# A mixture of retrieved experts: the v product in plain float32 on four column groups, per quarter of 64 tokens

## The chip, the cores and the metric

One core of one Trainium2 chip runs the whole program. The metric is the device time of one execution in microseconds (us). The engines are TensorE (PE for its matmuls, PEld for its weight loads), VectorE (DVE), ScalarE (ACT), GpSimd (POOL) and SyncE (SP); 16 DMA engines move data.

## The reference

One encoder layer over 256 tokens of width 2048 (mixer, then a retrieval layer, all float32). The change is in the retrieval layer and in what prepares it:

```python
def peer_ffn(h, w_q, sub_keys, u_tab, v_tab):
    ...                                   # 8 heads x 16 experts of 16384 chosen per token, with a gate g
    def token_block(args):
        hx, ids, g = args
        u = u_tab[ids]
        a = jnp.einsum('td,tnd->tn', hx, u)
        act = jax.nn.gelu(a, approximate=False) * g
        return jnp.einsum('tn,tnd->td', act, v_tab[ids])
```

The output is `x + gate2 * peer_ffn(h2)`, normalised once more. An expert that no token chose has weight zero for every token, so the sums may also run over all experts, token by token, with a weight matrix `act` that is mostly zero.

## The kernel before

**Stages.** The mixer runs first. Then the queries and keys of the retrieval; then the *u stage*: the 16384 experts in 128 blocks of 128, each block's `u` loaded (SP), split into a float32r part `hu` and a remainder `lu` (ACT copies, DVE subtracts, lines 154 and 155), and multiplied with the hidden state in 48 matmuls of 256 columns (lines 169 to 173). Beside it run, as steps of generators paced by declared costs (`pay`), the choice of the experts (`side_steps`) and, from block 51 on, `sort_steps`. The products, through gelu and times the gate, go to a table `actd` in DRAM, one row of 256 tokens per expert; the last two blocks (`TAIL`) stay on chip.

**The sort.** `gmax` holds, per token tile of 128, whether an expert has any weight there (built in `oh_use`). `sort_steps` gives each expert one of four classes (only tile 0, both, only tile 1, none), ranks experts by class with small matmuls, and inverts the rank into the index `perm_idx`: block `b` of the sorted order is a list of 128 expert numbers. Fixed limits (`T0_TO`, `T1_FROM`, `T1_TO`) say which blocks are multiplied for which tile; `miss` is 1 if a class does not fit its limits.

**The v stage**, the subject here. Sorted blocks 0 to 108 are gathered by POOL: 128 rows of `peer_v` (1 MB, `rv`, line 1085) and their 128 rows of `actd` (128 KB, `mc`, line 1147), each by an indirect DMA with `perm_idx`. Fetches run `AHEAD` = 6 blocks ahead of the products, in POOL's queue in program order. For each block `v_block` splits the raw values into hi (ACT, line 1102) and lo (DVE, line 1103), splits the weights `mc` likewise (lines 159, 160), and adds into eight PSUM banks `po`, four of 512 columns for each token tile, three products (hi hi, lo hi, hi lo) of 128x128 weights and 512 moving columns: 12 matmuls per block and tile (line 1114). Blocks 0 to 79 count for tile 0, 28 to 108 for tile 1, so 161 (block, tile) pairs; blocks for both tiles and for one alternate, and the last four are for tile 1 alone. The two tail blocks go first (12 matmuls per tile). Six blocks before the end stands a branch (`values_load` and `tc.If`, lines 1175 to 1177): if `miss` is set, all the block and tile pairs left out are added as well.

**The end.** For each tile: `po` times the gate plus the stored `x` (lines 1190, 1191), square and sum (1197), the root and its refinement (179 to 185), the gain (1203), the scale (1207, 1209), the store (1210).

**Column groups.** One place of the kernel already addresses the array in groups of 32 columns, in `ada_q` at the start (line 353): plain float32, 32 weight columns, 512 moving columns, four at a time with four different moving slices:

```python
PE.matmul(prow[32 * j:32 * j + 32], lhsT=cact[:, k:k + 1].to_broadcast([128, 32]),
          rhs=raw[:, j], start=(k == ADA_PE[j]), stop=(k == ADA_PE[j + 4]),
          tile_position=(0, 32 * j))
```

The matmul of line 903 is plain float32 on the full array, 128x128 weights and 512 columns.

Of the kernel before, what the change touches and what calls it, by code (L numbers as in the profile page):

```python
# [9 lines left out]
F32 = mybir.dt.float32  # L10
F32R = mybir.dt.float32r
# [17 lines left out]
NBLK = 128  # L29
# [10 lines left out]
HPV = 0  # L40
T0_TO = 80
T1_FROM = 28
T1_TO = 109
# [3 lines left out]
AHEAD = 6  # L47
# [39 lines left out]
def hybrid_block_kernel(  # L87
# [642 lines left out]

    def a8(name, shape=(128, 8, 256), dt=F32):
        return ap_.tile(list(shape), dt, tag="A", name=name, bufs=ABUFS)
# [54 lines left out]
    gmax = [work[:, 2048 + 128 * i:2176 + 128 * i] for i in range(2)]  # L787
    stages = {}

    def oh_make(tt, q):  # L790
        t = tt * 128 + q * 4
        it = iota.unsqueeze(1).to_broadcast([128, 4, 128])
        ohs = []
        for i, src in enumerate((i2T, i1T)):
            oh = e2(f"oh{tt}_{q}") if i else work[:, 2304 + 512 * ((32 * tt + q) % 3):][:, :512]
            oh = oh.rearrange("p (t i) -> p t i", t=4)
            V.tensor_tensor(oh, it, src[:, t:t + 4].unsqueeze(2).to_broadcast([128, 4, 128]), ALU.is_equal)
            ohs.append(oh)
        for j in range(4):
            S.activation(ohs[1][:, j], ohs[1][:, j], AF.Copy, scale=gT[:, t + j:t + j + 1])  # L800
        return ohs

    def oh_use(tt, q, ohs):
# [10 lines left out]
        if qq == TB // 4 - 1:  # L814
            S.dma_start(gd[tt * (128 // TB) + tb], stage)
            if tb == 0:
                V.tensor_reduce(gmax[tt], stage, AX.X, ALU.max)
            else:
                mx = e2(f"mx{tt}_{tb}")[:, :128]
                V.tensor_reduce(mx, stage, AX.X, ALU.max)  # L820
                V.tensor_tensor(gmax[tt], gmax[tt], mx, ALU.max)
# [87 lines left out]
    def sort_steps():  # L909
        tri = work[:, 0:128]  # L910
        V.tensor_scalar(tri, iota, pidx, None, ALU.is_gt)
        cls = work[:, 128:640].rearrange("p (c i) -> p c i", c=4)
        for tt in range(2):
            V.tensor_single_scalar(gmax[tt], gmax[tt], 0.0, ALU.is_gt)
            V.memset(gmax[tt][:, NBLK - TAIL:], 0.0)
        V.tensor_tensor(cls[:, 1], gmax[0], gmax[1], ALU.mult)
        V.tensor_tensor(cls[:, 0], gmax[0], cls[:, 1], ALU.subtract)
        V.tensor_tensor(cls[:, 2], gmax[1], cls[:, 1], ALU.subtract)
        V.tensor_tensor(cls[:, 3], gmax[0], cls[:, 2], ALU.add)
        V.tensor_scalar(cls[:, 3], cls[:, 3], -1.0, 1.0, ALU.mult, ALU.add)  # L920
        yield 3.0
        pt = ps_tile("clstot")
        for c in range(4):
            keep(PE.matmul(pt[:, c:c + 1], lhsT=cls[:, c], rhs=ones[:, 0:1], start=True, stop=True))
        yield 5.0
        tot = work[:, 1408:1416]
        keep(V.tensor_copy(tot[:, 0:4], pt[:, 0:4]))
        yield 3.0
        keep(PE.matmul(pt[:, 8:12], lhsT=ones, rhs=tot[:, 0:4], start=True, stop=True))
        yield 5.0  # L930
        keep(V.tensor_copy(tot[:, 4:8], pt[:, 8:12]))
        yield 3.0
        pr = ps_tile("rank")
        keep(PE.matmul(pr, lhsT=tri, rhs=cls.rearrange("p c i -> p (c i)"), start=True, stop=False,
                      skip_group_check=True))
        for c in range(4):
            for k in range(c + 1):
                keep(PE.matmul(pr[:, c * 128:(c + 1) * 128], lhsT=tot[:, k:k + 1].to_broadcast([128, 128]),
                              rhs=tri if k == c else ones, start=False, stop=(c == 3 and k == 3),
                              skip_group_check=True))  # L940
        yield 5.0
        rk = e2("rk")
        keep(V.tensor_tensor(rk, cls.rearrange("p c i -> p (c i)"), pr, ALU.mult))
        rank = work[:, 640:1024].rearrange("p (c i) -> p c i", c=3)
        V.tensor_reduce(rank[:, 0], rk.rearrange("p (c i) -> p i c", c=4), AX.X, ALU.add)
# [8 lines left out]
        lim = work[:, 1416:1420]  # L954
        V.tensor_scalar(lim[:, 0:1], tot[:, 4:5], -1.0, 128.0 * T1_FROM, ALU.mult, ALU.add)
        V.tensor_tensor(lim[:, 1:2], tot[:, 4:5], tot[:, 5:6], ALU.add)
        V.tensor_tensor(lim[:, 2:3], lim[:, 1:2], tot[:, 6:7], ALU.add)
        V.tensor_single_scalar(lim[:, 1:2], lim[:, 1:2], -128.0 * T0_TO, ALU.add)
        V.tensor_single_scalar(lim[:, 2:3], lim[:, 2:3], -128.0 * T1_TO, ALU.add)
        V.tensor_reduce(lim[:, 3:4], lim[:, 0:3], AX.X, ALU.max)  # L960
        V.tensor_single_scalar(lim[:, 3:4], lim[:, 3:4], 0.0, ALU.is_gt)
        V.tensor_copy(miss, lim[:, 3:4])
# [127 lines left out]
    turn = [0]  # L1090

    def hi_lo(name):
        k = turn[0]
        turn[0] += 1
        if k % 4 < 2:
            return [wp.tile([128, 2048], F32R, tag="w" + x, name=f"{x[0]}v{name}") for x in ("hi", "lo")]
        return spare[:, k % 2], cst.tile([128, 2048], F32R, tag="T3" + "ab"[k % 2], name=f"lv{name}")

    def v_block(raw, w, av, mm, tts, start=(), stop=()):
        hi, lo = w  # L1100
        with tc.high_priority(offset=HPV):
            S.activation(hi, raw, AF.Copy)  # L1102
            V.tensor_tensor(lo, raw, hi.bitcast(F32), ALU.subtract)  # L1103
        mh, ml = mm
        cs = slice(tts[0] * 128, (tts[-1] + 1) * 128)
        split_to(av[:, cs], mh[:, cs], ml[:, cs])
        for tt in tts:
            tsl = slice(tt * 128, (tt + 1) * 128)
            terms = list(enumerate(((mh, hi), (mh, lo), (ml, hi))))
            order = [(t, d4) for t in terms for d4 in range(4)]  # L1110
            if tt in stop:
                order = [(t, d4) for d4 in range(4) for t in terms]
            for (i, (lhs, rhs)), d4 in order:
                PE.matmul(po[tt * 4 + d4], lhsT=lhs[:, tsl], rhs=rhs[:, d4 * 512:(d4 + 1) * 512],  # L1114
                          start=(tt in start and i == 0), stop=(tt in stop and i == 2))

    units = []
    rest = []
    for b in range(NBLK):
        tts = [b < T0_TO, T1_FROM <= b < T1_TO]  # L1120
        units.append((b, [tt for tt in range(2) if tts[tt]]))
        rest.append((b, [tt for tt in range(2) if not tts[tt]]))
    both = [u for u in units if len(u[1]) == 2]
    ones_ = [u for u in units if len(u[1]) == 1]
    rest = [u for u in rest if u[1]]
    main = []
    late = ones_[-LATE:]
    ones_ = ones_[:-LATE]
    while both or ones_:
        if both:  # L1130
            main.append(both.pop(0))
        if ones_:
            main.append(ones_.pop(0))
    main += late

    tails = [v_raw(i - TAIL, f"d{i}") for i in range(TAIL)]
    raws, ms = [], []

    def fetch_raw(n):
        if n < len(main):  # L1140
            raws.append(v_raw(main[n][0], f"{main[n][0]}"))
# [6 lines left out]

    for n in range(AHEAD - TAIL):
        fetch_raw(n)  # L1150
    for n in range(AHEAD - TAIL):
        fetch_m(n)
    spare = None
    for i in range(TAIL):
        v_block(tails[i], hi_lo(f"d{i}"), ab[-1][:, ABLK - TAIL + i],
                [m1(f"m{x}d{i}", F32R) for x in "hl"], (0, 1), start=(0, 1) if i == 0 else ())
    final = {}
    for n, (b, tts) in enumerate(main):
        for tt in tts:
            final[tt] = n  # L1160
    spare = cst.tile([128, 2, 2048], F32R, tag="T1", name="hvs")
    gfin = None
# [3 lines left out]
    for n, (b, tts) in enumerate(main):  # L1166
        for k in ((AHEAD - TAIL + n * 2, AHEAD - TAIL + n * 2 + 1) if n < TAIL else (n + AHEAD,)):
            fetch_raw(k)
            fetch_m(k)
        if n % 4 == 0:  # L1170
            mm = wp.tile([128, 4, 2, 256], F32R, tag="wraw", name=f"mm{n}", bufs=WRAW)
        v_block(raws[n], hi_lo(f"{b}"), ms[n // 8][:, n % 8], (mm[:, n % 4, 0], mm[:, n % 4, 1]), tts,
                stop=[tt for tt in tts if final[tt] == n])
        if n == len(main) - 1 - AHEAD:
            flag = nc.values_load(miss[0:1, 0:1], min_val=0, max_val=1)
            xr = a8("xr", (128, 2048))
            with tc.If(flag > 0):
                xm = e2("xm")
                xs = [sp.tile([128, 512], F32R, tag="e2", name=f"xs{i}", bufs=E2BUFS) for i in range(2)]
                for rb, rtts in rest:  # L1180
                    nc.gpsimd.indirect_dma_start(xr, None, v_rows, index(rb))
                    nc.gpsimd.indirect_dma_start(xm[:, :256], None, actd[:, :], index(rb))
                    v_block(xr, hi_lo(f"x{rb}"), xm[:, :256], xs, rtts)
            gfin = a8("gfin", (128, 2048))
            nc.sync.dma_start(gfin, g_final.partition_broadcast(128))

# [37 lines left out]
def _consts():  # L1224
# [13 lines left out]
    mats = np.zeros((128, 2, 128), f)  # L1238
# [62 lines left out]
```

## Time and profile before

| | |
|---|---|
| median of 3 runs | 1894.97 us (1893.25 to 1897.15) |
| profiled execution, its own time | 1894.67 us |
| its span, first to last instruction | 1892.7 us |
| mean granted TensorE clock | 0.975 |
| TensorE / DVE / ACT / POOL busy | 95% / 73% / 49% / 20% |
| v stage, line 1114: first and last matmul start | 1414.4 and 1878.9 us |

Busy shares are means over the span; what a stage waits for has to be read in that stage. A matmul's record runs from its start to the end of its drain, so records overlap: the cost of one in a stream is the distance between starts, not its duration. A plain float32 matmul leaves two records.

### The profile page before, as it was taken

To read this page: it belongs to the slowest core of one execution; us is meant where nothing else is said; L and a number is where in the kernel's file an instruction comes from. 1 tells how busy PE (TensorE), PEld (TensorE's weight loads), DVE (VectorE), ACT (ScalarE), POOL (GpSimd) and SP (SyncE) were. 2 spreads that over 40 slices of the span, in tenths; PEclk is the share of its full clock that TensorE was granted. 3 is DMA by queue.
4 is the path that set the end of the run, shared out by engine and by line. 5 is a ranking of instruction groups with operands and counts; after the bars stand their busy time and mean duration, and the time that the engine had idled before them with its cause. 6 is when DMAs were issued, how large, how long until landed. Compare 5 with 4: busy or idle time off the path is not lost. (4 is left out here: it accounts for less than half of the span.)

```text
span 1892.7 us, 30584 instructions
## 1 busy us (share of the span) xinstructions
PE 1795.0 (95%) x12863; PEld 1675.1 (89%) x12863; DVE 1385.6 (73%) x1707; ACT 924.4 (49%) x1163; POOL 371.4 (20%) x257
## 2 busy tenths in 40 slices
PE   4878999899999998998999999999999999999995
PEld 2668999899999998998999999999998888888884
DVE  7568879888678977988657788876456665666666
ACT  3214457345544488578733334334345555555544
POOL 0000000000000000000000000000028887777760
PEclk8888999999999999999999999999999999999998
DMA  9976968789644555556597888888668888888781
GB/s 394 383 288 246 354 234 338 280 304 348 231 170 171 193 186 187 188 188 217 188 327 274 302 275 302 296 297 327 239 235 303 325 307 291 273 288 300 277 299 68
DMA packets 77794, 506.00 MB, mean 267 GB/s; under 512 B 9328, under 2 KB 9968, under 8 KB 22352
## 3 DMA queue, kind: packets, MB, share of 16 engines
q1 hardware_dynamic: 44640, 319.79, 45.5%
q0 software_dynamic: 29712, 162.94, 25.1%
q10 hardware_dynamic: 3296, 21.24, 2.8%
q8 instruction: 102, 1.67, 0.3%
q14 instruction: 44, 0.36, 0.1%
HBM read 466.18 MB, written 37.75 MB: 266 GB/s over the span
## 5 line engine op out<-in xcount | busy, mean ns | idle before, releaser
L169 PE MATMUL pu<-h2hi,hu 128*128 128x256 f32 x2048 | 500.3, 286 | 0.0
L154 ACT ACTIVATE hu<-ru 128x2048 fp32r<-128x2048 f32 x128 | 245.4, 1917 | 367.9 <-PE pu L170 326.0
L155 DVE TENSOR_TENSOR lu<-ru,hu 128x2048 fp32r<-128x2048 f32 x128 | 292.9, 2289 | 170.1 <-ACT hu L154 168.4
L169 PEld LDWEIGHTS pu<-h2hi,hu 128*128 128x128 f32 x2048 | 387.7, 189 | 0.6 <-issue 0.2
L173 PE MATMUL pu<-h2hi,lu 128*128 128x256 f32 x2048 | 263.0, 281 | 0.0
L170 PE MATMUL pu<-h2loT3a,hu 128*128 128x256 f32 x1024 | 252.0, 284 | 0.0
L173 PEld LDWEIGHTS pu<-h2hi,lu 128*128 128x128 f32 x2048 | 251.3, 188 | 0.0
L170 PE MATMUL pu<-h2loT3b,hu 128*128 128x256 f32 x1024 | 248.2, 281 | 0.0
L1013 POOL DMA_DIRECT2D gg<-gd x16 | 18.7, 1171 | 938.2 <-DMA gd<-stage 938.2
L170 PEld LDWEIGHTS pu<-h2loT3a,hu 128*128 128x128 f32 x1024 | 195.4, 191 | 0.2 <-issue 0.2
L170 PEld LDWEIGHTS pu<-h2loT3b,hu 128*128 128x128 f32 x1024 | 193.4, 189 | 0.0
L1147 POOL DMA_INDIRECT mc<-actd,perm_idx x109 | 184.3, 1691 | 33.2 <-issue 32.6
L1114 PE MATMUL po<-lv,mm 128*128 128x512 f32 x644 | 176.3, 394 | 1.4 <-DVE lv L1103 1.4
L1114 PE MATMUL po<-hvs,mm 128*128 128x512 f32 x648 | 170.0, 397 | 0.0
L1103 DVE TENSOR_TENSOR lv<-rv,hv 128x2048 fp32r<-128x2048 f32 x54 | 123.8, 2294 | 62.6 <-ACT hv L1102 61.0
L1114 PE MATMUL po<-hv,mm 128*128 128x512 f32 x640 | 164.7, 392 | 4.3 <-ACT hv L1102 4.3
L1103 DVE TENSOR_TENSOR lv<-rv,hvs 128x2048 fp32r<-128x2048 f32 x55 | 126.0, 2295 | 56.7 <-ACT hvs L1102 56.6
L1085 POOL DMA_INDIRECT rv<-in_peer_v_dram,perm_idx x109 | 153.1, 1405 | 62.2 <-issue 23.5
L1114 PEld LDWEIGHTS po<-hvs,mm 128*128 128x128 f32 x648 | 122.3, 189 | 29.4
L1114 PEld LDWEIGHTS po<-hv,mm 128*128 128x128 f32 x640 | 120.6, 189 | 30.5 <-ACT hv L1102 4.8
L1114 PEld LDWEIGHTS po<-lv,mm 128*128 128x128 f32 x644 | 121.4, 189 | 29.6 <-DVE lv L1103 2.0
L159 ACT ACTIVATE mm<-mc 128x256 fp32r<-128x256 f32 (+1 forms) x109 | 39.2, 361 | 191.9 <-DMA mc<-actd,perm_idx 191.8
(523 smaller groups left out, 3332.5 us busy)
## 6 DMA issues: line engine op xcount, KB each, us to landing
ru<-in_peer_u_dram SPq DMA_DIRECT2D x128, 1024.0 KB, 5.3
ada<-in_w_ada_dram SPq DMA_DIRECT2D x96, 1024.0 KB, 6.1
rwin<-in_w_in_dram SPq DMA_DIRECT2D x33, 1024.0 KB, 6.5
rwout<-in_w_out_dram SPq DMA_DIRECT2D x16, 1024.0 KB, 5.4
rwq<-in_w_q_dram SPq DMA_DIRECT2D x16, 1024.0 KB, 5.2
gd<-stage ACTq DMA_DIRECT2D x16, 1024.0 KB, 5.1
gg<-gd POOLq DMA_DIRECT2D x16, 1024.0 KB, 11.3
actd<-A POOLq DMA_DIRECT2D x15, 1024.0 KB, 6.4
```

The costliest lines, as they stand in the source:

```text
L154: S.activation(hi, raw, AF.Copy)
L155: V.tensor_tensor(lo, raw, hi.bitcast(F32), ALU.subtract)
L159: S.activation(hi, src, AF.Copy)
L169: PE.matmul(dst, lhsT=whi[:, sl], rhs=rhi[:, c], start=(c == sets[0][0]), stop=False)
L170: PE.matmul(dst, lhsT=whi[:, sl], rhs=rlo[:, c], start=False, stop=False)
L173: PE.matmul(dst, lhsT=wlo[:, sl], rhs=rhi[:, c], start=False, stop=(c == sets[-1][-1]))
L1013: keep(nc.gpsimd.dma_start(gg, gd[:, :, k * ABLK:(k + 1) * ABLK, :].rearrange("tb p i t -> p tb i t")))
L1085: keep(nc.gpsimd.indirect_dma_start(raw, None, v_rows, index(b)))
L1103: V.tensor_tensor(lo, raw, hi.bitcast(F32), ALU.subtract)
L1114: PE.matmul(po[tt * 4 + d4], lhsT=lhs[:, tsl], rhs=rhs[:, d4 * 512:(d4 + 1) * 512], start=(tt in start and i == 0), stop=(tt in stop and i ...
L1147: keep(nc.gpsimd.indirect_dma_start(ms[-1][:, n % 8], None, actd[:, :], index(main[n][0])))
```

## The change

It does five things.

1. **Products.** In the v stage, raw float32 values are used as they come from the DMA; the hi and lo parts, their tiles and the splits of the weights are gone. A product is made per sorted block and *quarter* of 64 tokens: the quarter's 64 weight columns are two groups of 32, each a matmul of 128x32 weights and 512 columns on its own column group of the array (`tile_position`), for four 512-column slices.
2. **Order.** A plan pairs a product of an even quarter (column groups 0, 1) with one of an odd quarter (groups 2, 3); the matmuls of a pair are issued slice by slice, four groups each. The blocks' order is chosen so that even and odd products keep level and about one block is used per pair.
3. **Sort.** `gmax` is kept per quarter, experts fall in 15 classes (every non-empty set of quarters) in the order of `QCLASSES`, whose pairs are the block windows allowed for each class. Compares, totals, ranks and limits follow; class tables and matmuls are bfloat16.
4. **Buffers.** Raw blocks use 11 buffers (7 `A`, 4 `wraw`) with fetches 8 ahead and 5 before the tails; the tails are loaded into `wraw` by SP; `xr` and `gfin` use the freed `whi`.
5. **The branch** stands where the fetches have all been asked for, and the last two pairs are merged slice by slice, so that the PSUM banks finish one after the other.

```diff
-T0_TO = 80
-T1_FROM = 28
-T1_TO = 109
+QCLASSES = ((7, 0, 6), (5, 4, 13), (13, 10, 17), (9, 15, 24), (1, 22, 36), (3, 32, 42), (2, 40, 53),
+            (10, 51, 60), (11, 57, 65), (15, 62, 68), (14, 66, 73), (6, 70, 80), (4, 77, 91),
+            (12, 88, 98), (8, 95, 109))
+NSORT = max(hi for _, _, hi in QCLASSES)
-AHEAD = 6
+EARLY = 5
+AHEAD = 8
+RAWS = 11
...
+        for k in range(nk):
+            V.tensor_single_scalar(cls[:, k], key, float(order[k]), ALU.is_equal)
+        yield 4.0
...
+        for k4 in range(0, nk, 4):
+            pr = ps_tile(f"rank{k4}")
+            keep(PE.matmul(pr, lhsT=tri, rhs=cls[:, k4:k4 + 4].rearrange("p k i -> p (k i)"), start=True, stop=False,
+                          skip_group_check=True))
+            for k in range(4):
+                keep(PE.matmul(pr[:, k * 128:(k + 1) * 128], lhsT=tot[:, k4 + k:k4 + k + 1].to_broadcast([128, 128]),
+                              rhs=tri, start=False, stop=(k == 3), skip_group_check=True))
+            yield 5.0
...
-    def v_block(raw, w, av, mm, tts, start=(), stop=()):
-        hi, lo = w
-        with tc.high_priority(offset=HPV):
-            S.activation(hi, raw, AF.Copy)
-            V.tensor_tensor(lo, raw, hi.bitcast(F32), ALU.subtract)
...
+    late = [u for u in steps if u[1] == 3][-2:] + [u for u in steps if u[1] == 12][-LATE:]
...
+    def halves(need):
+        return [q for q in (0, 2) if need >> q & 1], [q for q in (1, 3) if need >> q & 1]
...
+    def product(raw, m, q, d4, stop=False):
+        for s in range(2):
+            g, j = 2 * q + s, 2 * (q % 2) + s
+            bank = q // 2 * 4 + d4
+            PE.matmul(po[bank][32 * j:32 * j + 32], lhsT=m[:, 32 * g:32 * g + 32],
+                      rhs=raw[:, d4 * 512:(d4 + 1) * 512], start=(bank, j) not in seen, stop=stop,
+                      tile_position=(0, 32 * j))
+            seen.add((bank, j))
+
+    def v_raw(n, name):
+        if n % RAWS in (2, 5, 8, 10):
+            return wp.tile([128, 2048], F32, tag="wraw", name=f"rv{name}", bufs=WRAW)
+        return a8(f"rv{name}", (128, 2048))
...
     for i in range(TAIL):
...
+        for q0 in (0, 2):
+            for d4 in range(4):
+                for q in (q0, q0 + 1):
+                    product(tails[i], ab[-1][:, ABLK - TAIL + i], q, d4)
...
+    while i < n_pairs:
+        group = pairs[i:i + 1] if i < n_pairs - 2 else pairs[i:]
+        fetch_to(max(n for p in group for n, _ in p) + AHEAD)
+        for d4 in range(4):
+            for k, p in enumerate(group):
+                for n, q in p:
+                    product(raws[n], ms[n // 8][:, n % 8], q, d4, stop=ends[q] == i + k)
+        if i == at_if:
             flag = nc.values_load(miss[0:1, 0:1], min_val=0, max_val=1)
...
```

## Rows read from the trace of the kernel before

**Rows 1.** Part 1 of the page: busy us (share of the span) and instructions.

```profile
PE 1795.0 (95%) x12863; PEld 1675.1 (89%) x12863; DVE 1385.6 (73%) x1707; ACT 924.4 (49%) x1163; POOL 371.4 (20%) x257
```

**Rows 2.** Stretches: us, busy (count) of PE, PEld, DVE, ACT, POOL, PEclk, DMA share, GB/s.

```profile
1250.00:1300.00 50.00, 50.00 (x426) 49.68 (x424) 36.49 (x28) 18.30 (x18) 4.08 (x4) 1.00 0.81 282
...
1414.00:1854.00 440.00, 439.99 (x1913) 358.48 (x1911) 272.00 (x215) 228.12 (x215) 333.28 (x215) 1.00 0.83 294
1854.00:1880.00 26.00, 19.61 (x72) 15.07 (x72) 23.45 (x28) 15.85 (x18) 0.00 (x0) 0.87 0.01 3
```

**Rows 3.** Line 1114: count, duration ns min/median/max, first and last start.

```profile
L1114 PE MATMUL po<-hvs,mm x648: 395/396/628, 1425.3 to 1878.9; 128*128 128x512 f32 x162
...
L1114 PE MATMUL po<-hvd,mhd x16: 389/389/398, 1414.4 to 1423.3; 128*128 128x512 f32 x16
```

**Rows 4.** Order of time, PE around the If: start, us, instruction, wait before.

```profile
1852.92 1.07 PE L1114 MATMUL po<-hv,mm 128*128 128x512 f32 x4
1858.32 1.35 PE L1114 MATMUL po<-hv,mm 128*128 128x512 f32 x4 [4.33 <-ACT hv L1102]
1861.05 2.08 PE L1114 MATMUL po<-lv,mm 128*128 128x512 f32 x4 [1.38 <-DVE lv L1103]
```

**Rows 5.** DMA from 1430 to 1840 us: packets, MB, share; issues, landing us.

```profile
q0 software_dynamic: 19773, 121.50, 83.7%
...
rv<-in_peer_v_dram,perm_idx POOLq DMA_INDIRECT x104, 6.5
mc<-actd,perm_idx POOLq DMA_INDIRECT x103, 5.2
```

**Rows 6.** Order of time, PE and PEld near 46 and 53 us.

```profile
46.61 0.16 PEld L353 LDWEIGHTS adarow<-ada,cact 128*32 128x32 f32 x8
46.61 1.06 PE L353 MATMUL adarow<-ada,cact 128*32 128x512 f32 x8
...
47.61 0.39 PE L625 MATMUL pin<-hhi,hwin 128*128 128x256 f32 x1
...
53.48 1.92 PE L353 MATMUL adarow<-ada,cact 128*32 128x512 f32 x16
```

**Rows 7.** Order of time, PE at line 903.

```profile
1359.84 3.60 PE L903 MATMUL gtfp<-gtf,ones 128*128 128x512 f32 x8
```

**Rows 8.** POOL's gathers, lines 1085 and 1147: duration ns, starts.

```profile
L1085 POOL DMA_INDIRECT rv<-in_peer_v_dram,perm_idx x109: 933/944/3035, 1408.9 to 1839.2; - x109
...
L1147 POOL DMA_INDIRECT mc<-actd,perm_idx x109: 942/996/3066, 1414.9 to 1840.5; - x109
```

**Rows 9.** Groups by line in the u stage, and the index's last step.

```profile
L970 PE MATMUL inv<-sv,sl 128*128 128x256 bf16 x128 | 19.5, 275 | 0.0
...
L155 DVE TENSOR_TENSOR lu<-ru,hu 128x2048 fp32r<-128x2048 f32 x74 | 169.5, 2290 | 133.5 <-ACT hu L154 131.7 <-ACT A L1045 1.6 <-PE inv L970 0.2
...
L993 DVE CAST perm_idx<-work x1: 228/228/228, 1294.8 to 1294.8; 128x128 uint32<-128x128 f32 x1
```

**Rows 10.** Order of time, the end of the kernel.

```profile
1881.89 1.28 DVE L1191 TENSOR_TENSOR oacc<-oacc,ev 128x512 f32<-128x512 f32 x2
...
1883.24 0.58 ACT L1197 ACTIVATE po<-oacc 128x512 f32<-128x512 f32 x1
1883.76 0.19 ACT L1197 ACTIVATION_READ_ACCUMULATOR po<-oacc 128x1 f32 x1
1884.90 0.15 DVE L1199 TENSOR_REDUCE fsum<-fs 128x1 f32<-128x4 f32 x1
...
1886.76 1.15 ACT L1207 ACTIVATE oacc<-oacc,fr1r 128x1024 f32<-128x1024 f32 x1 [0.81 <-DVE fr1r L185]
...
1887.94 0.34 ACTq L1210 DMA_DIRECT2D out_dram<-oacc  x1
```

**Rows 11.** Line 353: duration ns of its weight loads.

```profile
L353 PEld LDWEIGHTS adarow<-ada,cact x128: 105/108/178, 19.9 to 140.8; 128*32 128x32 f32 x128
```

**Rows 12.** Order of time, PE from 19 us.

```profile
19.94 3.34 PE L353 MATMUL adarow<-ada,cact 128*32 128x512 f32 x16
```

More of the change, by code (lines that the diff above doesn't have):

```diff
@@ L786, in hybrid_block_kernel @@
     work = cst.tile([128, 4096], F32, tag="T2", name="work")
-    gmax = [work[:, 2048 + 128 * i:2176 + 128 * i] for i in range(2)]
+    gmax = [work[:, 2048 + 128 * i:2176 + 128 * i] for i in range(4)]
     stages = {}
@@ L921, in sort_steps @@
         yield 3.0
+        for k in range(nk):
+            V.tensor_single_scalar(cls[:, k], key, float(order[k]), ALU.is_equal)
+        yield 4.0
         pt = ps_tile("clstot")
-        for c in range(4):
-            keep(PE.matmul(pt[:, c:c + 1], lhsT=cls[:, c], rhs=ones[:, 0:1], start=True, stop=True))
+        for k in range(nk):
+            keep(PE.matmul(pt[:, k:k + 1], lhsT=cls[:, k], rhs=ones_bf[:, 0:1], start=True, stop=True))
         yield 5.0
-        tot = work[:, 1408:1416]
-        keep(V.tensor_copy(tot[:, 0:4], pt[:, 0:4]))
+        keep(V.tensor_copy(tot, pt[:, 0:nk]))
@@ L928, in sort_steps @@
         yield 3.0
-        keep(PE.matmul(pt[:, 8:12], lhsT=ones, rhs=tot[:, 0:4], start=True, stop=True))
+        keep(PE.matmul(pt[:, 32:32 + nk], lhsT=ones_bf, rhs=tot, start=True, stop=True))
         yield 5.0
-        keep(V.tensor_copy(tot[:, 4:8], pt[:, 8:12]))
-        yield 3.0
[L933 to L945, printed above, removed]
+        ends = [work[:, 1440 + nk * i:1440 + nk * (i + 1)] for i in range(2)]
+        sums = work[:, 1440 + 2 * nk:1440 + 3 * nk]
+        keep(V.tensor_copy(sums, pt[:, 32:32 + nk]))
+        src = sums
+        for i, d in enumerate((1, 2, 4, 8)):
+            V.tensor_copy(ends[i % 2][:, :d], src[:, :d])
+            V.tensor_tensor(ends[i % 2][:, d:], src[:, d:], src[:, :nk - d], ALU.add)
+            src = ends[i % 2]
@@ new lines, in sort_steps @@
+        starts = ends[0]
+        V.tensor_tensor(starts, src, sums, ALU.subtract)
+        over = work[:, 1664:1696]
+        V.tensor_tensor(over[:, 0:nk], lims[:, 0:nk], starts, ALU.subtract)
+        V.tensor_tensor(over[:, nk:2 * nk], src, lims[:, nk:2 * nk], ALU.subtract)
+        V.tensor_reduce(work[:, 1696:1697], over, AX.X, ALU.max)
+        V.tensor_single_scalar(work[:, 1696:1697], work[:, 1696:1697], 0.0, ALU.is_gt)
+        V.tensor_copy(miss, work[:, 1696:1697])
+        yield 3.0
@@ new lines, in sort_steps @@
+        rank = work[:, 1664:2048].rearrange("p (c i) -> p c i", c=3)
+        for k4 in range(0, nk, 4):
[6 more added lines that the diff above has]
+            yield 5.0
+            rk = e2(f"rk{k4}")
+            for k in range(4):
+                op = V.scalar_tensor_tensor(rk[:, k * 128:(k + 1) * 128], pr[:, k * 128:(k + 1) * 128],
+                                            starts[:, k4 + k:k4 + k + 1], cls[:, k4 + k], ALU.add, ALU.mult)
+                if k == 0:
+                    keep(op)
+            dst = rank[:, 1] if k4 else rank[:, 0]
+            V.tensor_reduce(dst, rk.rearrange("p (c i) -> p i c", c=4), AX.X, ALU.add)
+            if k4:
+                V.tensor_tensor(rank[:, 0], rank[:, 0], rank[:, 1], ALU.add)
@@ L1117, in hybrid_block_kernel @@
[L1117 to L1124, printed above, removed]
+    steps = []
+    for b in range(NSORT):
+        need = 0
+        for m, lo, hi in QCLASSES:
+            if lo <= b < hi:
+                need |= m
+        steps.append((b, need))
@@ L1125, in hybrid_block_kernel @@
+    rest = [(b, 15 & ~(steps[b][1] if b < NSORT else 0)) for b in range(NBLK)]
     rest = [u for u in rest if u[1]]
+    late = [u for u in steps if u[1] == 3][-2:] + [u for u in steps if u[1] == 12][-LATE:]
+    left = [u for u in steps if u not in late]
     main = []
[L1127 to L1133, printed above, removed]
-    main += late
-    tails = [v_raw(i - TAIL, f"d{i}") for i in range(TAIL)]
+    odd = taken = 0
@@ new lines, in halves, with unlike @@
+    def halves(need):
+        return [q for q in (0, 2) if need >> q & 1], [q for q in (1, 3) if need >> q & 1]
+    while left:
+        def unlike(u):
+            e, o = halves(u[1])
+            return (abs(odd + len(o) - len(e)) + abs(2 * (len(main) + 1) - taken - len(e) - len(o)), u[0])
+        u = min(left, key=unlike)
+        left.remove(u)
+        e, o = halves(u[1])
+        odd += len(o) - len(e)
+        taken += len(e) + len(o)
+        main.append(u)
+    main += late
+    pairs = []
@@ new lines, in hybrid_block_kernel @@
+    for part in (range(len(main) - len(late)), range(len(main) - len(late), len(main))):
+        lanes = [[(n, q) for n in part for q in halves(main[n][1])[i]] for i in range(2)]
+        for i in range(max(len(x) for x in lanes)):
+            pairs.append([lane[i] for lane in lanes if i < len(lane)])
+    n_pairs = len(pairs)
+    seen = set()
+    def product(raw, m, q, d4, stop=False):
[6 more added lines that the diff above has]
+            seen.add((bank, j))
@@ L1137, in hybrid_block_kernel @@
+    def v_raw(n, name):
+        if n % RAWS in (2, 5, 8, 10):
+            return wp.tile([128, 2048], F32, tag="wraw", name=f"rv{name}", bufs=WRAW)
+        return a8(f"rv{name}", (128, 2048))
+    tails = []
+    for i in range(TAIL):
+        raw = load_raw(peer_v[NBLK - TAIL + i], f"rvd{i}")
+        tails.append(raw)
     raws, ms = [], []
@@ L1147, in fetch_m @@
             keep(nc.gpsimd.indirect_dma_start(ms[-1][:, n % 8], None, actd[:, :], index(main[n][0])))
-    for n in range(AHEAD - TAIL):
+    for n in range(EARLY):
         fetch_raw(n)
-    for n in range(AHEAD - TAIL):
+    for n in range(EARLY):
         fetch_m(n)
-    spare = None
     for i in range(TAIL):
[L1155 to L1162, printed above, removed]
+        for q0 in (0, 2):
+            for d4 in range(4):
+                for q in (q0, q0 + 1):
+                    product(tails[i], ab[-1][:, ABLK - TAIL + i], q, d4)
     oacc = cst.tile([128, 2, 2048], F32, tag="T2", name="oacc")
@@ L1165, in hybrid_block_kernel, with fetch_to @@
         nc.sync.dma_start(oacc[:, tt], xd[tt])
[L1166 to L1174, printed above, removed]
+    gfin = None
+    asked = EARLY
+    at_if = next(i for i, p in enumerate(pairs) if max(n for n, _ in p) + AHEAD >= len(main) - 1)
+    ends = {}
+    for i, p in enumerate(pairs):
+        for n, q in p:
+            ends[q] = i
+    def fetch_to(n):
+        nonlocal asked
+        while asked <= min(n, len(main) - 1):
+            fetch_raw(asked)
+            fetch_m(asked)
+            asked += 1
+    i = 0
+    while i < n_pairs:
[3 more added lines that the diff above has]
+            for k, p in enumerate(group):
+                for n, q in p:
+                    product(raws[n], ms[n // 8][:, n % 8], q, d4, stop=ends[q] == i + k)
+        if i == at_if:
             flag = nc.values_load(miss[0:1, 0:1], min_val=0, max_val=1)
[L1176 removed]
+            xr = load_tile("xr")
             with tc.If(flag > 0):
                 xm = e2("xm")
[L1179 to L1180 removed]
+                for rb, need in rest:
                     nc.gpsimd.indirect_dma_start(xr, None, v_rows, index(rb))
                     nc.gpsimd.indirect_dma_start(xm[:, :256], None, actd[:, :], index(rb))
[L1183 to L1184 removed]
+                    for q in range(4):
+                        if need >> q & 1:
+                            for d4 in range(4):
+                                product(xr, xm[:, :256], q, d4)
+            gfin = load_tile("gfin")
             nc.sync.dma_start(gfin, g_final.partition_broadcast(128))
+        i += len(group)
     def add_up(po, j, tt, name):
```

71 lines of the change are left out of this document (26 added, 45 removed).

## The prediction

> **What bounds the kernel now.** I read the page's busy shares first. TensorE is busy 95% of the span, no other engine more than 73% [rows 1]; so the question for each stage is whether TensorE waits there. The table by stretches comes next. In the u stage and from 1414 to 1854 us TensorE is busy the whole time at the full granted clock (1.00, the 2.4 GHz level) [rows 2]. The first v matmul starts at 1414.4 and the last at 1878.9 [rows 3]; with 0.40 us for the last one the v stage is 464.9 us long. Its cost is a plain rate: 1913 matmuls in 440 us are 0.230 us each, and 161 (block, token tile) pairs x 12 plus 48 for the two tail blocks are 1980, so 455.4 us. The other 9.5 us lie at 1854 to 1866: TensorE stops after the If (4.33 us until ACT's hi, then 1.38 until DVE's lo) and four matmuls then take 2.08 us where they took 1.07 before, at a granted clock of 0.87 for the stretch [rows 2, 4]. Thirdly the DMA: 83.7% of its engines' time in the v stage [rows 5], so not the bound, but the next one. The end, from 1879.3 to 1892.7, is 13.4 us of DVE, ACT and the store.
>
> **What replaces the matmuls.** Twelve float32r matmuls per block and 128 tokens become, per block and quarter, eight float32 matmuls of 32 columns: two column groups x four 512-column slices. Even quarters (0, 2) use groups 0 and 1, odd ones (1, 3) groups 2 and 3, so a pair of one even and one odd product gives four sets of four matmuls side by side. Counting the class windows by the diff's own loop, the quarters need 53, 54, 53 and 57 blocks: 106 even, 111 odd, hence 111 pairs, five of them with the odd half alone (same time). With the tails, 2 blocks x 2 pairs x 4 sets, there are 111 x 4 + 16 = 460 sets.
>
> **The price of a set.** The trace has this operation elsewhere: line 353 runs plain float32 128x512 on four column groups of 32, each group with its own moving data. Eight records (each float32 matmul leaves two) span 1.06 us, and a run of sixteen spans 1.92 [rows 6]: the second set adds 0.86. A float32 matmul on the full array, line 903, takes 3.60 us for four [rows 7], so the four groups really run at once. I take 0.86 us: 460 x 0.86 = 395.6 us. Below, the same sixteen records leave no room under about 0.85; above, the single set's 1.06 if nothing overlaps between sets, which is one of the rivals.
>
> **The splits go.** 109 ACT copies, as many DVE subtractions and the small splits vanish from the stage. They ran beside TensorE, so this by itself gives nothing, except where TensorE waited for them: the 4.33 and 1.38 us behind the If, and the half-rate matmuls after. What is late there next is the branch alone: TensorE's queue must run empty and refill. No row isolates that; it lies between 0.3 and 4.3 us [rows 4]. I take 1, since the 4.33 is put down to ACT's hi, which is gone. Stage: 395.6 + 1.0 = 396.6 us, 68.3 less.
>
> **DMA.** The blocks fetched stay 109, a row gather of 1 MB and one of 128 KB each. From 1430 to 1840, 104 and 103 of them took 83.7% of 410 us, 343 us, 3.32 us a block at full use [rows 5]. A pair takes 3.44 us and the plan uses about one block per pair, so the DMA would be some 95% busy and TensorE stay ahead of nothing: 109 x 3.32 = 362 us against 111 x 3.44 = 382. The gathers begin at 1408.9 as now [rows 8]; the tails keep TensorE until 1414.4 + 13.8 = 1428.2, by when 5.8 blocks fit and one is needed. The 11 raw buffers let POOL ask eight ahead. POOL's issues take 0.94 to 1.00 us at the median and up to 3.1 [rows 8]; 218 of them at 1.25 with the 0.3 between are 272 us, so its queue does not bind. Nothing else waits behind them on POOL. What the deeper look-ahead costs the DMA no row shows: at worst the cadence of today, 410/103.5 = 3.96 us a block, at best 3.32.
>
> **Start, sort, end.** The tails' loads use the weight buffers of the last u blocks on SP's queue instead of A buffers; they need no split, and their first product still waits for u block 127 on TensorE, so 1414.4 stays. The sort adds on DVE 16 compares, 16 PSUM multiplies and 3 more reductions, some 13 us, in a stretch where DVE stands idle 133.5 us for ACT's hi [rows 9]: nothing. On TensorE, which is full there, 37 small bf16 matmuls replace 16 float32 ones: between -3 and +3 us by the 0.15 us of the inversion's matmul (19.5 us for 128 [rows 9]); I take 0. Its steps declare 19 more units at 2 a block, so the index is ready some ten blocks (54 us) later than 1294.8 [rows 9]: 1349, still before the first gather at 1408.9. At the end DVE no longer carries splits: token tile 0 is finished four pairs (13.8 us) before the last, so after the last bank come two DVE steps (1.28), the square and its read (0.77), the chain from the sum to the scale (1.86), the scale (1.18) and the store (4.76) [rows 10], 9.9 us for 13.4. I take 3.5 off; from 0 to 4.
>
> **Sum.** Against the profiled execution's own 1894.67 us (span 1892.7 and 2.0 around it; the median of the runs, 1894.97, is the same within 0.02%): -68.3 - 3.5 = -71.8, so 1823 us.
>
> **The rivals.**
> *Loads and matmuls cannot issue that fast.* A set is eight weight loads and eight matmuls in 0.86 us, 107 ns a couple. The longest dense stream of the trace, the u stage, has 426 matmuls in 50 us, 117 ns a couple [rows 2]. Sixteen couples in a row did go at 107 [rows 6], but from a filled queue. If 117 is a floor, a set is 0.94: 432 us, 1860.
>
> *The DMA binds.* At 3.96 us a block the last block lands near 1408.9 + 432 = 1841, TensorE ends at 1845 and the kernel takes 1857; at 3.64 TensorE just keeps up. For it: 95% use leaves little; against: eight blocks in flight, and today's idle DMA time is the wait for buffers that TensorE frees.
>
> *Slower: a set pays its fill and its weight loads anew.* The place is the boundary between rounds in every set. If the loads (105 to 178 ns [rows 11]) do not go beside the running round, a set costs the single one's 1.06 us: 460 x 1.06 + 1 = 488.6, 23.7 more than now, less 3.5: 1915. It decides from 1.015 us a set. For it: the next matmul after a lone set comes 1.00 us after its start [rows 6]. Against: the 1.92 for two sets, and the eight loads of the lone set done in 0.16 us while its first round ran. The Trainium skill speaks for this rival ("TensorE: Matmul & The Clock Gate", Part 3, Packing small matmuls): there a weight load goes beside a running matmul only when the row groups differ, and here all four column groups use the same 128 rows. By that rule the time would be the 1915 just worked out; the trace's second set at 0.86 disagrees with it, so I give it little.
>
> *The change doesn't do what it says.* If a class lies outside its window, the If is taken and 295 more block-quarters follow, over 1,000 us at four sets each. Counted from the reference's own selection for its inputs, the 15 classes end at blocks 4.7, 11.6, 16.4, 23.1, 34.1 and so on up to 107.8 of 109, each inside its window by half a block or more: 1%.
>
> Half clock is the rest: line 353's first sets, after an idle TensorE, took 3.34 us for sixteen records [rows 12]. Here TensorE comes from a full stream, so I leave it within the slower 7%.
>
> **How the numbers follow.** As forecast 67% (1814 to 1832: the If, the sort and the end at their bounds), issue floor 14%, DMA 11%, slower 7%, taken If 1%. The range runs from 1814 to 1862, taking in the issue floor and the DMA case. About 0.2% (4 us) is what a measurement of this kernel can tell from no change; only a set of 1.01 to 1.02 us lands there, 1%. Faster 91%, same 1%, slower 8%.
>
> **What would show it.** Right: v matmuls of 128x32 form in rounds 0.43 us apart, two rounds a set; the first v matmul near 1414 and the last near 1811; DMA share above 0.9 in the stage; no ACT or DVE work there; a gap near 1 us at the If; 10 us after the last matmul. Wrong: rounds 0.47 or 0.53 apart; TensorE waiting for the raw gather or the mc gather in the waits; a granted clock under 1.00 in the stage; a first v matmul later than 1414.

## The result and the profile after

The changed kernel took 1840.95 us (median of four executions, 1839.73 to 1842.11) where the kernel before, on the same chip, took 1895.18: a ratio of 0.9714, 95% interval 0.9697 to 0.9731. The forecast was 1823. Loaded anew later, the same kernel took 1820.21, 1820.80 and 1839.29 us; most of the experiments are about these two levels.

Part 1 of the profiled execution's page (span 1840.3 us), which answers to [rows 1]: DVE and ACT have lost the splits, TensorE's share is as before.

```profile
PE 1743.8 (95%) x14485; PEld 1471.9 (80%) x14488; DVE 1109.2 (60%) x1529; ACT 682.4 (37%) x941; POOL 240.4 (13%) x257
```

The product's line in the changed kernel is 1155. Its records, with count, duration in ns and first and last start, answer to [rows 3]:

```profile
L1155 PE MATMUL po<-rv,mc x3472: 589/592/617, 1426.5 to 1828.9; 128*32 128x512 f32 x193
L1155 PE MATMUL po<-rvd,A x128: 589/592/617, 1409.2 to 1427.0; 128*32 128x512 f32 x128
```

The stage starts 5.2 us earlier than before and is 420.2 us long, by the last start and 0.43 us; 396.6 were forecast. Now three stretches of it by engine (columns as in [rows 2]):

```profile
1412.00:1418.00 6.00, 5.39 (x26) 1.08 (x22) 0.00 (x0) 0.00 (x0) 2.98 (x4) 1.00 1.01 426
1429.00:1445.00 16.00, 13.97 (x92) 3.97 (x88) 0.00 (x0) 0.00 (x0) 9.74 (x11) 1.00 1.02 403
1540.00:1660.00 120.00, 120.00 (x1124) 65.39 (x1120) 0.00 (x0) 0.00 (x0) 63.70 (x68) 1.00 0.91 341
```

The reader should read the counts, not the busy time. A stretch counts every record that touches it. Of the 1124 in the third, 1117 begin in its 120 us, which is 0.86 us for eight: the forecast's set. In the first, TensorE is "busy" 5.39 of 6 us with 26 records, where the same place of a loading without stops, below, has 64: for most of it the matmuls run one at a time instead of four side by side, and a busy share can't show that. The granted clock is 1.00 in all three. ACT and DVE do nothing.

The order of time around the If, which answers to [rows 4]. The releaser named here, a gather, is doubtful: the other loadings name TensorE's own queue, below.

```profile
1786.46 3.17 PE L1155 MATMUL po<-rv,mc 128*32 128x512 f32 x25
1791.52 1.05 PE L1155 MATMUL po<-rv,mc 128*32 128x512 f32 x4 [1.90 <-DMA rv<-in_peer_v_dram,perm_idx]
```

The DMA from 1430 to 1825 us, which answers to [rows 5]:

```profile
q0 software_dynamic: 19577, 120.24, 81.1%
...
rv<-in_peer_v_dram,perm_idx POOLq DMA_INDIRECT x101
mc<-actd,perm_idx POOLq DMA_INDIRECT x101
```

The end in order of time, which answers to [rows 10]:

```profile
1828.43 1.05 PE L1155 MATMUL po<-rv,mc 128*32 128x512 f32 x4
...
1829.83 0.69 DVE L1236 TENSOR_TENSOR ev<-po,gtf 128x512 f32<-128x512 f32 x1
...
1830.43 0.68 DVE L1249 TENSOR_TENSOR oacc<-oacc,gfin 128x512 f32<-128x512 f32 x1
1831.03 0.69 DVE L1237 TENSOR_TENSOR oacc<-oacc,ev 128x512 f32<-128x512 f32 x1
1831.81 0.60 ACT L1243 ACTIVATE po<-oacc 128x512 f32<-128x512 f32 x1 [1.68 <-DVE oacc L1237]
...
1834.43 1.15 ACT L1253 ACTIVATE oacc<-oacc,fr1r 128x1024 f32<-128x1024 f32 x1 [0.81 <-DVE fr1r L187]
...
1835.61 0.34 ACTq L1256 DMA_DIRECT2D out_dram<-oacc  x1
```

From 1829.5 to 1840.3 it is 10.8 us, for 13.4 before and 9.9 forecast.

Against the profiled execution's own 1842.11 us: start and end together are 4.3 us better than forecast (-5.2 and +0.9), the stage 23.6 worse, and what lies outside the span 0.2 shorter. The question is the stage. Its losses lie in places: the tails; 1430 to 1439; then single stops of 1.4 to 1.9 us, at 1469, 1499, 1528, 1667, 1697, 1756 and 1766. In the tails starts lie 0.70 us apart, between 1430 and 1439 0.71 or 1.41, and no semaphore wait is shown there: the waits put them down to "issue".

### The profile page after: what moved, and what is told of

Same layout as the page of the kernel before. It is cut to its first block, busy times and chain, and to the rows that moved or that the text cites. A ratio compares the mean times of both kernels' runs of the same rounds, so it can differ in the third digit from the quotient of the medians.

```text
span 1840.3 us, 33209 instructions
## 1 busy us (share of the span) xinstructions
PE 1743.8 (95%) x14485; PEld 1471.9 (80%) x14488; DVE 1109.2 (60%) x1529; ACT 682.4 (37%) x941; POOL 240.4 (13%) x257
## 4 chain that ended last, share of the span: by engine, by line
PE 81%; DVE 7%; ACT 5%; issue 3%; DMA 2%; POOL 1%; SPq 0%; DVEq 0%; ACTq 0%; POOLq 0%
PE po L1155 19%; PE pu L172 12%; PE pu L171 12%; PE pu L175 12%; DVE lwin L157 2%; PE pq L171 2%; PE pq L175 2%; PE pq L172 2%; ACT oh L805 2%; PE gps L815 2%; DMA rv<-in_peer_v_dram,perm_idx 2%; PE pwin L171 2%; PE pwin L172 1%; PE pwout L171 1%; PE pwout L172 1%
## 5 line engine op out<-in xcount | busy, mean ns | idle before, releaser
L1155 PE MATMUL po<-rv,mc 128*32 128x512 f32 x3472 | 396.3, 592 | 6.6 <-issue 3.5
L1155 PEld LDWEIGHTS po<-rv,mc 128*32 128x32 f32 x3472 | 170.0, 110 | 232.2 <-issue 199.1
L1236 DVE TENSOR_TENSOR ev<-po,gtf 128x512 f32<-128x512 f32 x8 | 5.4, 686 | 404.2 <-PE po L1155 404.2
L1180 POOL DMA_INDIRECT mc<-actd,perm_idx x109 | 103.3, 948 | 100.8 <-PE po L1155 58.3
L1174 POOL DMA_INDIRECT rv<-in_peer_v_dram,perm_idx x109 | 103.1, 946 | 87.6 <-PE po L1155 40.0
L199 DVE SCALAR_TENSOR_TENSOR acc<-ada,cact,acc 128x2048 f32<-128x2048 f32 x45 | 105.6, 2347 | 5.1 <-DMA ada<-in_w_ada_dram 5.1
L156 ACT ACTIVATE hwin<-rwin 128x2048 fp32r<-128x2048 f32 x33 | 63.1, 1915 | 85.2 <-DMA rwin<-in_w_in_dram 41.7
L805 ACT ACTIVATE oh<-oh,gT 128x128 f32<-128x128 f32 x256 | 81.0, 392 | 22.8 <-DVE oh L802 22.3
L171 PE MATMUL pwin<-hhi,hwin 128*128 128x256 f32 x336 | 84.7, 292 | 0.0
L815 PE MATMUL gps<-oh,work 128*128 128x128 f32 x512 | 69.9, 284 | 13.0 <-ACT oh L805 12.9
```

What stands on the lines that cost most here:

```text
L171: PE.matmul(dst, lhsT=whi[:, sl], rhs=rhi[:, c], start=(c == sets[0][0]), stop=False)
L199: V.scalar_tensor_tensor(acc, raw, cact[:, k:k + 1], acc, ALU.mult, ALU.add)
L815: keep(PE.matmul(p[:, j * 128:(j + 1) * 128], lhsT=ohs[0][:, j], rhs=ohs[1][:, j], start=True, stop=True))
L1155: PE.matmul(po[bank][32 * j:32 * j + 32], lhsT=m[:, 32 * g:32 * g + 32], rhs=raw[:, d4 * 512:(d4 + 1) * 512], start=(bank, j) not in seen, ...
L1174: keep(nc.gpsimd.indirect_dma_start(raws[n], None, v_rows, index(main[n][0])))
L1180: keep(nc.gpsimd.indirect_dma_start(ms[-1][:, n % 8], None, actd[:, :], index(main[n][0])))
```

## The experiments

The kernels ran in four series. Within a series all ran on one chip beside the kernel before; the record numbers the four chips 1, 4, 12 and 12, and whether a number stands for the same chip in two series is not known. "Loading" below means a program loaded for one series.

**Series 1: is it the supply of instructions, or the data?** Kernel before: 1895.52 us.

*cols64.*

```
-for s in range(2): PE.matmul(po[bank][32*j:32*j+32], lhsT=m[:, 32*g:32*g+32], ..., tile_position=(0, 32*j))
+j = q % 2
+PE.matmul(po[bank][64*j:64*j+64], lhsT=m[:, 64*q:64*q+64], ..., tile_position=(0, 64*j))
```

> One matmul of 64 columns where the change has two of 32, so half the matmuls and half the weight loads for the same columns of moving data: 230 rounds pairs at the same 0.86 us, 1800 records for 3600. Theory A (TensorE's supply of instructions makes the stalls of 1.0 to 1.4 us that come every 29.4 us, and the slow tails): the stalls come half as often or go, the v stage is 400 to 410 us for 420.3, the kernel 1822 to 1832 us for 1841. Theory B (the data come late, DMA share 0.99 to 1.01 in the first slices): the stalls and the start stay, 1839 to 1843. Theory C (a weight load goes beside a running matmul only because other column groups are free): with two groups instead of four a load of 64 columns shows, a set goes from 0.86 to 1.0 us or more, 1890 or more.

Measured: 1821.28 us, ratio 0.9606 (0.9582 to 0.9631), stage 401.0.

*half256.*

```
+for c in (0, 256):
+    PE.matmul(po[bank][32*j:32*j+32, c:c+256], ..., rhs=raw[:, d4*512+c:d4*512+c+256], ...)
```

> Each matmul of 512 moving columns cut into two of 256: the same columns, twice the matmuls and weight loads (7200 records). Theory A (supply of instructions): 32 instructions in 0.86 us can't be had; if the u stage's 117 ns for a load and a matmul is near the ceiling, the v stage takes 3600 couples... 3680 pairs of load and matmul over what a queue gives, 700 us or more, the kernel 2100 us or more; the stalls come twice as often. Theory B (late data): matmuls still fill the array, 1841 to 1850.

Measured: 1828.14 us, 0.9644 (0.9621 to 0.9667), stage 407.1. The stretch from 1540 to 1660 us, first of cols64, then of half256:

```profile
1540.00:1660.00 120.00, 120.00 (x562) 48.26 (x560) 0.00 (x0) 0.00 (x0) 68.18 (x73) 1.00 0.92 349
```

```profile
1540.00:1660.00 120.00, 120.00 (x2232) 103.90 (x2224) 0.00 (x0) 0.00 (x0) 67.74 (x72) 1.00 0.92 347
```

562, 1124 and 2232 records: the same columns in the same time, at 9, 19 and 37 instructions a us (loads counted). Theory A in its first form, a ceiling on the rate, falls: twice the change's rate is sustained for 120 us. half256's stage is 8.4 us longer than that of the change without stops (398.7, series 2). Its hole at the If (5.1 us for 1.8) is the largest piece, and why it is longer there stays open; some 2.4 us more are lost behind the hole, where the granted clock is 0.50 from 1776.8 to 1781.0 us, and the rest is spread over the stage. Theory C falls too: with only two column groups the loads (132 to 137 ns) are hidden as well.

*halfdma.*

```
+if n % 2:
+    raws.append(raws[n - 1])
+    return
 raws.append(v_raw(n, ...))
```

> Every second block's raw rows are not gathered, the block before is used in their place (part of the data is left out, so the output is another): 55 raw gathers for 109, the matmuls unchanged. Theory A: the stalls of 1.0 to 1.4 us each 29.4 us stay, the start's DMA waits (2.8 and 1.9 us) go: 1833 to 1838 us. Theory B: stalls and start go, the stage is 400 us or less, 1820 to 1826.

Measured: 1824.88 us, 0.9623 (0.9598 to 0.9648), stage 402.7, of which 5.0 are the hole at the If. The time fits Theory B, but cols64 and half256, with all their data, lost the stalls as well: it can't be told from this run. The waits of 2.8 and 1.9 us that the expectation puts at the start stand at the If in the first loading's trace (1791.5). Behind its hole this run shows what the change's shorter ones (1.6 to 2.0 us, granted clock 1.00) do not, the half clock:

```profile
1774.40:1779.60 5.20, 5.20 (x14) 1.35 (x16) 0.00 (x0) 0.00 (x0) 0.00 (x0) 0.50 0.02 3
```

Six rounds there start 0.82 us apart where 0.43 is usual: 2.4 us, so without the hole and the half clock the stage is 395.3.

*noif.*

```
-flag = nc.values_load(miss[0:1, 0:1], ...)
-with tc.If(flag > 0): ...            # the fallback
```

> The If and its fallback are left out (the blocks outside the class windows would not be added if there were any; here there are none). Both theories: the 2.1 to 2.5 us hole at the If goes, and one refill of TensorE's queue with it: 1837.5 to 1839.5 us for 1841. If the whole 24 us beyond 460 sets came from the branch and what it does to the code's layout, 1820.

Measured: 1816.87 us, 0.9587 (0.9563 to 0.9611), stage 395.4: 24 us below the first loading of the change. A hole of 2.5 us can't give that. TensorE's instructions are the same up to the If, and the tails' stop, some 370 us ahead of it, is gone as well. The stage is within 0.2 us of the forecast's 395.6 for the 460 sets alone. So either the series or any edit at all had done away with the stalls, and the missing run was the change itself.

**Series 2: the change again.** Kernel before: 1897.52 us.

*same* (no edit).

> The change's kernel once more, word for word. Its profile lost about 20 us in stalls that none of cols64, half256, halfdma and noif shows (their stages: 401.0, 407.1, 402.7 and 395.4 us for 420.2), though noif's TensorE instructions are the same ones up to the If. Theory D (the stalls belong to that loading of the program, not to its code): 1817 to 1824 us, a v stage near 400. Theory E (the stalls belong to this code as built, and each of the four edits happens to break them): 1839 to 1843, a stage near 420.

Measured: 1820.21 us (1818.91 to 1822.25), 0.9605 (0.9572 to 0.9638): the interval lies clear of the first loading's. Theory D holds, E falls. The same kernel, stretch for stretch, in this loading, then its waits of TensorE from 1400 to 1830 us (us, times, longest):

```profile
1412.00:1418.00 6.00, 6.00 (x64) 1.81 (x60) 0.00 (x0) 0.00 (x0) 2.84 (x3) 1.00 1.01 423
1429.00:1445.00 16.00, 16.00 (x152) 5.83 (x148) 0.00 (x0) 0.00 (x0) 12.18 (x13) 1.00 1.01 408
1540.00:1660.00 120.00, 120.00 (x1124) 43.97 (x1119) 0.00 (x0) 0.00 (x0) 68.09 (x73) 1.00 0.93 350
```

```profile
PE po L1155 <- PEq L1220: 1.8, 1, 1.8
PE po L1155 <- DMA mc<-actd,perm_idx: 1.6, 1, 1.6
```

64 records for 26 and 152 for 92, at the same DMA share (1.01) and clock. The data were no earlier here: it is this loading that waits 1.6 us for them. Matmul for matmul, the first loading falls behind this one by:

```
tails 3.6 (of which 1.8 come back, the gate gather being waited for here)   1427 to 1447 us: 6.8
1462 to 1549 us: 5.7        1549 to 1661: -0.3        1661 to 1770: 7.0        the If: 0.5
sum 21.5 = 420.2 - 398.7 us
```

*inter.*

```
 for n in range(EARLY):
     fetch_raw(n)
-for n in range(EARLY):
     fetch_m(n)
```

> The first five raw gathers and five gate gathers are asked for in turns (raw, gate, raw, gate) instead of five raws and then five gates, so the first product has its gates 4 MB earlier. Theory B (start late by data): the start's wait for the gate gather (1.6 to 2.8 us) goes, 1 to 3 us less than the same kernel without it. Theory D: 1816 to 1822 in all; theory E: 1836 to 1841 if the stalls stay, 1820 if any edit breaks them.

Measured: 1819.23 us, 0.9599 (0.9566 to 0.9633), stage 396.8 for 398.7: the wait for the gate gather is gone from TensorE's waits, as expected, and the 1 us in all can't be told from nothing.

*tiles.*

```
 need |= m
+need |= (3 if m & 3 else 0) | (12 if m & 12 else 0)
```

> Each block's product is taken for both quarters of a token tile if either needs it (their gates are zero, so the output is the same): 162 pairs for 111, all with four groups. What plain float32 on four groups would give with the tile classes' work of before. 51 pairs x 4 sets x 0.86 us = 175 us more: 1994 to 1999 us if the stage without them is 400, 2012 to 2018 if it is 420. That is 100 us slower than before, if the sorting by quarters carries the whole gain; rival: 1895 or less, if the format alone does.

Measured: 1996.03 us, 1.0527 (1.0491 to 1.0564), 175.8 more than same. Its product's records:

```profile
L1155 PE MATMUL po<-rv,mc x5184: 589/592/617, 1426.2 to 1983.6; 128*32 128x512 f32 x200
```

5184 records are 162 pairs x 32, at the same price. Plain float32 on four groups, with as many products as the token tiles ask for (162 pairs, for 161 before), loses 98.5 us to the kernel before in its series; leaving out the quarters that need no product wins 176 back. So the format alone is no gain. The sorting by quarters in the old format was not run.

**Series 3: a third loading.** Kernel before: 1895.05 us.

*same2* (no edit).

> The change's kernel a third time, loaded anew. The first time it took 1840.95 us with stalls of multiples of 0.70 us in TensorE's stream that no wait explains, the second time 1820.21 without one. Theory D (they belong to a loading or a chip): either 1818 to 1823 with none, or 1839 to 1843 with the same stalls again near the tails and each 29.4 us. Theory F (they come and go from execution to execution): times of the single executions spread over 1818 to 1842 within this run.

Measured: 1820.80 us (1818.74 to 1822.67), 0.9612 (0.9588 to 0.9635), TensorE's waits in the stage 2.0 us for its queue at the If and 1.5 for the gate gather, no stalls. F falls: executions of a loading agree.

*cols64_inter* (both edits above).

> One matmul of 64 columns for two of 32, and the first raw and gate gathers in turns: the version with half of TensorE's instructions. If the supply of instructions is short in this loading (same2 near 1841), it loses less by it: 1820 to 1830. If not (same2 near 1820), the instructions are hidden anyway and only the start's 1.6 to 2 us go: 1817 to 1820.

Measured: 1822.22 us, 0.9625 (0.9597 to 0.9653). In this loading half the instructions give nothing. Since it never ran in a loading with stalls, whether it would cure them was not tried.

*ahead4.*

```
-EARLY = 5
-AHEAD = 8
+EARLY = 4
+AHEAD = 4
```

> Gathers asked for four blocks ahead instead of eight, four before the tails instead of five, nothing else. The prediction left open what the deeper look-ahead does. If the DMA has slack (0.88 share in the middle of the stage) and four blocks in flight carry it, the same time as same2 within 3 us. If the eight are needed to ride over stretches of full DMA share, TensorE waits for raw gathers and the time is 10 to 30 us more. If a deep DMA queue is what starves TensorE of instructions, the stalls are fewer here than in same2.

Measured: 1820.21 us, 0.9605 (0.9579 to 0.9631), the stage 396.7 us from 1413.0 to 1809.7. Four blocks in flight carry it, and the DMA doesn't bind. What a shallow queue does to the stalls is open, since same2 had none.

**Series 4: the stalls again.** Kernel before: 1893.85 us.

*same3* (no edit).

> The change's kernel in a fourth loading, beside it. 1840.95 us in the first, 1820.21 and 1820.80 in the second and third. Theory D: near 1820 or near 1841, with the stalls only in the second case; three of four near 1820 would make the first the exception.

Measured: 1839.29 us (1838.05 to 1840.54), 0.9712 (0.9684 to 0.974), the stage 418.6 us. Stretches of it (its stage starts at 1406.6, 2.5 us earlier than in the first loading):

```profile
1410.00:1416.00 6.00, 5.09 (x32) 1.44 (x28) 0.00 (x0) 0.00 (x0) 2.82 (x3) 1.00 1.01 422
1427.00:1443.00 16.00, 12.96 (x81) 4.06 (x76) 0.00 (x0) 0.00 (x0) 10.00 (x11) 1.00 1.00 400
1540.00:1660.00 120.00, 120.00 (x1124) 51.43 (x1120) 0.00 (x0) 0.00 (x0) 65.08 (x70) 1.00 0.90 337
```

```profile
PE po L1155 <- issue: 4.6, 9, 0.8
PE po L1155 <- PEq L1220: 1.6, 1, 1.6
```

The same kind of stops at the same places of the program, within a dozen records: against same it falls behind by 1.2 us to the end of the tails, 7.8 more by its 260th record (6.8 in the first loading), nothing from 1545 to 1658, and 19.9 in all. Two of the four loadings have them; within each, its executions (four and two) agree in time.

*cut128.*

```
-for d4 in range(4):   ... rhs=raw[:, d4 * 512:(d4 + 1) * 512]
+for d4 in range(16):  ... rhs=raw[:, d4 * 128:(d4 + 1) * 128]     # bank d4 // 4, columns of 128
```

> Each matmul of 512 moving columns cut into four of 128, the four groups in turns: the same columns, four times the matmuls and loads (14400 records), 74 instructions a us if the array stays full; half256 kept it full at 37. To see where the supply of instructions ends, and what a starved stream looks like. If 74 a us can be had: stage 400 to 410 us, 1820 to 1835. If the ceiling lies between: the stage is the number of instructions over it, at 50 a us 580 us and 2000 in all; and if the stalls of the first loading were a starved stream, starts lie apart by multiples of 0.70 us here too, with no wait shown.

Measured, in the series of same3: 2060.61 us, 1.088 (1.0849 to 1.0912). The stretch from 1540 to 1660, and the order of time near 1501:

```profile
1540.00:1660.00 120.00, 101.34 (x2848) 85.70 (x2842) 0.00 (x0) 0.00 (x0) 38.65 (x41) 0.94 0.59 213
```

```profile
1500.13 1.23 PE L1155 MATMUL po<-rv,mc 128*32 128x128 f32 x21
1501.67 0.43 PE L1155 MATMUL po<-rv,mc 128*32 128x128 f32 x6 [0.31 <-issue]
1502.42 0.44 PE L1155 MATMUL po<-rv,mc 128*32 128x128 f32 x7 [0.32 <-issue]
```

This reads as a starved stream: six or seven matmuls come together, then nothing for about 0.75 us from start to start, the releaser "issue", with the DMA share at 0.59. For stretches of up to 7 us it runs at the full 74 a us, on the mean at 47, a small part of the loss being the clock (0.94). The stalls of the first loading look the same (starts in steps of 0.70 us, no wait). It was not run in a loading without stalls, so its mean says nothing of those.

## Why the prediction was right, and by what it missed

**The two levels have to be judged apart.** 1820.21 and 1820.80 lie in the forecast's own case (1814 to 1832) and came about by its mechanism; that they are so near 1823 is partly luck, since in same a start 5.5 us early pays for 2 us more of stage and 1 us more of end. 1840.95 and 1839.29 lie outside that case. They are inside the whole range only because it was widened for an issue floor and for the DMA, and neither came about as described: there the hit is luck.

**The set (0.86 us): right.** 0.86 us (0.857 to 0.860 by the records that begin from 1540 to 1660 us) in all loadings of the change, for the second set's 0.86 in [rows 6]. The single set's 1.06 never appears in the full stream, so the slower rival falls: the weight loads (106 to 110 ns) go beside the running rounds. The Trainium skill ("TensorE: Matmul & The Clock Gate", Part 3, Packing small matmuls) says in its list of what overlaps that a load goes beside a matmul only when the row groups differ, though the same part also lets a load for the background weight buffer be pulled ahead. This case's trace disagrees with the list, with 1124 records and 1120 loads of the same 128 rows in 120 us.

**460 sets: right.** 3472 and 128 records are 460 x 8 less 80, the five pairs with one half of 16 records each.

**The If (1 us): mis-sized by one.** TensorE's queue takes 1.8, 2.0 and 1.6 us to run empty and refill (same, same2, same3), and the first loading's hole is 1.9; without the If it is gone (noif).

**DMA: not the bound, as forecast.** 81.1% of 395 us for 101 blocks are 3.17 us a block, under the 3.32. The DMA share above 0.9 that was to show this holds in the middle of the stage (0.91), not on its mean. The early gathers cost 1.6 us at the first product, which the forecast left out ("5.8 blocks fit and one is needed" counted the raw rows; five raw gathers stand ahead of the first gate gather, and inter, which takes them in turns, has no such wait; noif, in the old order, has 0.3).

**The start (stays at 1414.4): off by 5, to the good.** The first v matmul comes between 1406.6 and 1410.4 in the change's four loadings. Matmul for matmul of the u stage, the first loading gains 3.0 us on the kernel before between 700 and 800 us, 3.4 between 915 and 973 and 4.3 from there to 1120, where the sort's small matmuls lie, and gives 3.6 back between 1200 and 1400. No run isolates it, and of the kernel before there is one execution to compare.

**The end (9.9): 10.8.** Between DVE's two steps for the last bank stands a multiplication of another slice (1830.43, 0.68 us), which the sum didn't have.

**The issue-floor rival: false as a rate, and the term that is missing.** The forecast weighed a floor of 117 ns a load and matmul; half256 runs at 54 ns. But a stream this dense can stop: in two loadings of four it loses 20 to 21.5 us, in the others nothing. The sum without it (398.7 us of stage in same for 396.6) is good to 2 us, and its total of 1823 was met within 3 by 1820.21 and 1820.80; the 1840.95 is that plus the stalls. That instructions come late is the reading of the 0.70-us steps, of "issue" and of cut128; it is not shown directly. Late data are excluded: the DMA shares are equal, and same waits for data where the first loading does not; the code is excluded, being the same.

The trace holds more on the instructions. Part 3 of the page has a DMA queue of the kind "instruction" (packets, MB, share); first the change's line, then half256's:

```profile
q8 instruction: 115, 1.88, 0.4%
q8 instruction: 143, 2.34, 0.5%
```

half256 has 7200 instructions of TensorE more (3600 matmul records and as many loads) and 28 packets more, so each packet brings TensorE some 257 instructions, 16 KB. The first loading's stops at 1469, 1499 and 1528, and those at 1667 and 1697, stand 257 to 259 matmul records apart, with their loads two packets; cut128's groups mostly one or two. That ties the stops to the supply of instructions. But a late packet is not seen: the one ahead of the stop at 1469 begins at 1464.6 and takes 1.0 us, and none moves from 1466 to 1480. Which part of the supply stops stays open.

What a loading decides (where a program lies, which chip it gets) stays open too. If number 12 is one chip, the chip alone does not decide, since same2 ran on it without stops and same3 with them. All ten programs timed beside the kernel before in series 1 to 3 ran without, so it may go by the series; the two series with stops had the fewest programs (two and three, for four and five), and no run varies that. The kernel before, with half the instructions a us in this stage (17 a us in its u stage [rows 2]), shows no sign of it in its times: its medians in the five series are 1893.85 to 1897.52.

No version beat the change by more than can be told: inter at 1819.23 and noif at 1816.87, which gives up the fallback, are the lowest.

## What to carry to other kernels

Price a dense stream by the second of two sets in a row in the trace, not by one set alone: that gave the stage to within 2 us where the stream did not stop. Where engines work side by side in one unit, count records per us; a busy share hides matmuls that run one at a time. Before a loss of 1% is explained by the code, load the same kernel again: here two of the kernel's four loadings had it.

## What was not expected of the hardware

Matmuls of 64 columns on two column groups cost the same per column as 32 on four, loads hidden in both (562 and 1124 records in 120 us). TensorE kept 37 instructions a us for 120 us without a stop (half256), yet at 19 a us stopped in some loadings. In cut128 the granted clock was 0.68 from 1420 to 1440 us, a mean between its two levels (1.2 and 2.4 GHz), after 20 us in which TensorE was busy 16.16:

```profile
1400.00:1420.00 20.00, 16.16 (x158) 14.52 (x156) 4.81 (x4) 2.69 (x4) 10.47 (x11) 0.98 0.62 235
1420.00:1440.00 20.00, 16.84 (x343) 14.80 (x346) 0.00 (x0) 0.00 (x0) 7.55 (x8) 0.68 0.98 389
```
